# 108 extra TensorE products behind the last real one, with forward or backward moving operand and weights at step one or two

## The chip, the cores and the metric

The kernel runs on one core of one Trainium2 chip. That core has a TensorE for matrix products (PE in the profile, with its weight loads as PEld), VectorE (DVE), ScalarE (ACT), GpSimd (POOL) and SyncE (SP), which mostly issues transfers. Products read two operands from the on-chip memory SBUF, a weight block of up to 128 columns that is loaded into the array and a moving operand that streams past it, and write into PSUM, which has eight banks. The metric is the device time of one execution in microseconds (us); less is better.

## The reference

A decoder trunk of two layers on 256 tokens of width 1024, in float32. Layer 0 mixes tokens by forgetting attention, layer 1 by block-sparse attention with a shared position bias; each is followed by a SwiGLU network and a gated embedding. A final norm closes it.

```python
def reference(x, p, ...):
    h = x
    for i in range(DEPTH):
        u = _rmsnorm(h, attn_norm_g[i])
        ...
        h = h + _merge_heads(o) @ w_o[j]
        u = _rmsnorm(h, ffn_norm_g[i])
        gu = u @ ffn_w_in[i]
        h = h + (jax.nn.silu(gu[..., :D_FF]) * gu[..., D_FF:]) @ ffn_w_out[i]
        gate = jax.nn.sigmoid(_rmsnorm(h, ple_norm_g[i]) @ ple_w_gate[i])
        h = h + gate * (p[i] @ ple_w_up[i])
    return _rmsnorm(h, final_norm_g)
```

The change concerns the last two lines for layer 1, the gate and the final norm.

## The kernel before

For the large matrices, every float32 operand is split into two rounded parts, a high one and a rest (`hi` and `lo`), and every product of two such operands is made as three TensorE products into the same bank: high by high, high by low, low by high. That is `mm3` (lines 98 to 102); its three products appear in the profile as L100, L101 and L102. ScalarE makes the high part of a weight tile (`whi`, L188), VectorE the rest (`wlo`, L189), from a tile `raw` that SyncE fetches. The normed activations of a stage are the tile `g`: for each of 8 feature blocks 256 high values and behind them 256 low ones.

A weight tile is made by `half(at)` (line 144). It holds 1024 weights per partition in a tile that is 128 elements longer, and `at` says how many elements from the tile's start they begin. Where they begin differs by stage: `blocks` uses 16 (`APART`), the last stage 48.

The last stage is `ple` for layer 1 (from line 836 on). Its gate product is computed with tokens as rows: 128 tokens of `g` are the weights of the array, and the gate's matrix is the moving operand. First come the columns 0 to 511 for both token halves, in bank pairs `bks[0]`; then the columns 512 to 1023 for the first 128 tokens at 512 columns a product (`pair_unit` with `bks[1]`); then those for the second 128 tokens in two quarters of 256 columns (`tokens`, into `bks[1][1]` and into the bank `own`, named `pg_own` in the profile). Behind the last quarter stand six products into the bank `uown` (`pu_own`), the embedding's part of that quarter. The four weight tiles of this stage are the list `wts`; `nm.both` is `g`.

When a quarter is done, `part(t, i)` applies the gate (ScalarE's sigmoid, L844, VectorE's products and sums, L845 and L846), sums the squares for the final norm (L868 or L890) and multiplies by the last gain. `root` takes the root on GpSimd (L905), the rows are scaled (L912, L914, L928 to L932) and stored (`rows`, L902). All PSUM tiles come from one pool of eight banks in rotation (`bank`). Engines run in the order in which the program is written, apart from places where `tc.issue_after(x)` holds a piece back until `x` has been issued; the order of TensorE's last products is fixed in this way. At the end of the program (L1046) all engines meet in a barrier.

The extra products of the change read `wts[1]` as weights and `g` as moving operand.

Of the kernel before, what the change touches and what calls it, by code (L numbers as in the profile page):

```python
# [15 lines left out]
P = 128  # L16
S = 256
# [45 lines left out]
APART = 16  # L63
# [10 lines left out]
    ((2, 8), (0, 0), 0), ((0, 0), (2, 8), 64)  # L74
FORMS = {(_l, 0, _j): _HI2 for _l in range(2) for _j in (0, 4, 6)}
FORMS.update({(_l, "wo", _n): _HI2 for _l in range(2) for _n in (0, 2, 4)})
AGAIN = tuple((f, 0) for f in range(4, SEVEN + 4, 2))


# [2 lines left out]
def trunk(ctx: ExitStack, tc: tile.TileContext, pt, w, cst, gf, out):  # L82
# [7 lines left out]
    def bank(name):  # L90
        return ps.tile([P, 512], F32, tag="bank", name=name)
# [4 lines left out]
    mm = nc.tensor.matmul  # L96

    def mm3(o, a, b, start, stop):
        (ah, al), (bh, bl) = a, b
        mm(o, ah, bh, start=start, stop=False, skip_group_check=True)  # L100
        mm(o, ah, bl, start=False, stop=False, skip_group_check=True)  # L101
        return mm(o, al, bh, start=False, stop=stop, skip_group_check=True).ins  # L102
# [108 lines left out]
    def blocks(entry=False, form=None):  # L211

        if form:
            return half(APART, 0, form)
        hi, lo = half(APART, ENTRY * P if entry else 0)
        hi = [hi[:, k * P:(k + 1) * P] for k in range(KT)]
        return hi, lo if entry else [lo[:, k * P:(k + 1) * P] for k in range(KT)]
# [78 lines left out]
    nm = Norm(0)  # L296
# [9 lines left out]
    first = [half() for _ in range(EARLY)]  # L306
# [18 lines left out]
    def tokens(o, x, t, w, start, stop):  # L325

        at = slice(t * P, (t + 1) * P)
        return mm3(o, (x[0][:, at], x[1][:, at]), w, start, stop)

    def pair_unit(bks, c, wt, x, ts=(0, 1), mid=None):  # L330

        for kk in range(2):
            k = 2 * c + kk
            if kk and mid:
                mid()
            for t in ts:
                tokens(bks[t], x(k), t, [w[:, kk * HC:(kk + 1) * HC] for w in wt], k == 0, k == KT - 1)
# [252 lines left out]
    def ffn(layer, nm, filler, np_):  # L590
# [3 lines left out]
        def up(fs):  # L594
# [25 lines left out]
            for a in range(2):  # L620
                wt = blocks(form=_BOTH1 if (fs[0], a) in AGAIN else None)
                for k in range(KT):
# [152 lines left out]
    token = {}  # L775
# [60 lines left out]
    def ple(layer, nm, ut, nx):  # L836
# [4 lines left out]
        def gate(bk, t, c0, c1, u=None):  # L841
            at = slice(c0, c1)
            sg = work.tile([P, HC], F32, tag="t2k", bufs=3, name=f"pgt{layer}_{t}_{c0}")[:, 0:c1 - c0]
            nc.scalar.activation(sg, bk[:, c0 % HC:(c1 - 1) % HC + 1], AF.Sigmoid, scale=nm.col[:, t:t + 1])  # L844
            nc.vector.tensor_tensor(sg, sg, ut[:, t, at] if u is None else u, op=ALU.mult)  # L845
            nc.vector.tensor_tensor(h[:, t, at], h[:, t, at], sg, op=ALU.add)  # L846
# [17 lines left out]
        def square(t, i, c0, c1):  # L864

            sq = work.tile([P, S], F32, tag="sg", name=f"sqf{t}_{i}") if i else \
                work.tile([P, HC], F32, tag="t2k", bufs=3, name=f"sqf{t}_{i}")
            nc.scalar.activation(sq[:, 0:c1 - c0], h[:, t, c0:c1], AF.Square, scale=D ** -0.5,  # L868
                                 accum_out=ss[:, t, i:i + 1])

        for t in range(2):
# [3 lines left out]
        wts = [half(3 * APART) for _ in range(4)]  # L875
        uraw, uhi, ulo = [work.tile([P, 2, S], F32R if i else F32, tag="qkt", bufs=4, name=f"u{i}") for i in range(3)]
        nc.sync.dma_start(uraw, bass.AP(tensor=w.tensor, offset=w.offset + w_at(UP) + HC + S,
                                        ap=[[HW, P], [P * HW, 2], [1, S]]))
        with tc.issue_after(begun):
            split(uhi, ulo, uraw)  # L880
        uown = bank("pu1_own")
        own = bank(f"pg{layer}_own")

        def part(t, i):
            c0 = HC + i * S
            at = slice(c0, c0 + S)
            gate(own if t and i else bks[1][t], t, c0, c0 + S, uown[:, 0:S] if t and i else None)
            if t:
                sq = work.tile([P, S], F32, tag="sg", name=f"sqf1_{1 + i}")
                nc.vector.tensor_tensor_reduce(sq, h[:, t, at], h[:, t, at], 1.0 / D, ms[:, t, i:i + 1],  # L890
                                               ALU.mult, ALU.add, col[:, 1:2] if i else ms[:, t, 1:2])
            else:
                square(t, 1 + i, c0, c0 + S)
                if i:
                    nc.gpsimd.tensor_tensor(col[:, 0:1], ss[:, t, 2:3], ms[:, t, 1:2], op=ALU.add)
                else:
                    nc.vector.tensor_tensor(ms[:, t, 1:2], ms[:, t, 0:1], ss[:, t, 1:2], op=ALU.add)
            if not (t and i):
                nc.vector.tensor_tensor(ys[:, t, at], h[:, t, at], gb[:, at], op=ALU.mult)
# [4 lines left out]
        def root(t):  # L904
            nc.gpsimd.tensor_tensor(col[:, t:t + 1], col[:, t:t + 1], nhalf[:, 0:1], op=ALU.pow)  # L905

        for c in range(4):
            pair_unit(bks[1], c, wts[c], nm.k, (0,))
        part(0, 0)
# [6 lines left out]
        for i in range(2):  # L916
            for k in range(KT):
                c0 = (k % 2) * HC + i * S
                done = tokens((own if i else bks[1][1])[:, i * S:(i + 1) * S], nm.k(k), 1, [w[:, c0:c0 + S] for w in wts[k // 2]],
                       k == 0, k == KT - 1)  # L920
            if i:
                with tc.issue_after(done):
                    for k in range(2):
                        tokens(uown[:, 0:S], [p[:, k] for p in token["p"]], 1, (uhi[:, k], ulo[:, k]), k == 0, k == 1)
            part(1, i)
        root(1)
        r = col[:, 1:2]
        nc.scalar.activation(ys[:, 1, 0:HC], ys[:, 1, 0:HC], AF.Copy, scale=r)  # L928
# [6 lines left out]
    for layer in range(2):  # L935
        nf = Norm(3 * layer + 1)
        if layer == 0:
            attention(0, nm, fox_bias, first, nf)
        else:
            attention(1, nm, lambda _: (lambda: moba[2]), [], nf)  # L940
        got = []
        np_ = Norm(3 * layer + 2)
        ffn(layer, nf, lambda pp=None: ple_in(layer) if pp is None else got.append(ple_up(layer, pp)), np_)
        nm = Norm(3) if layer == 0 else None
        ple(layer, np_, got[0], nm)
# [104 lines left out]
```

## Time and profile before

| | us |
|---|---|
| median of 2 runs | 638.59 (638.58 to 638.59) |
| the profiled execution, its time | 638.56 |
| the profiled execution, its span from first to last instruction | 636.4 |

The profile is one execution. Its page gives the busy time of each engine, the chain of work that ended last, and groups of instructions. A group is named by line, engine, operation, what it writes and what it reads, and its shape. The timeline lists instructions with their start and duration in us, and in brackets how long the engine had idled and for whom. Products of TensorE overlap: a row's duration runs from its start to a modelled end, so the pace of a series is the distance between the starts. "SPq" rows are issues on SyncE's queue, and "DMA issues" give the time from an issue to its landing.

| engine | busy us | share of the span |
|---|---|---|
| TensorE, products | 629.4 | 99% |
| TensorE, weight loads (beside the products) | 608.4 | 96% |
| VectorE | 515.2 | 81% |
| ScalarE | 402.7 | 63% |
| GpSimd | 16.3 | 3% |

### The profile page before, as it was taken

The page shows a single profiled execution, that of the slowest core. Times are in us where ns is not written, and L with a number is a line of the kernel's source. Part 1 is how long each engine was busy: PE and PEld are TensorE (multiplying, and loading weights), DVE is VectorE, ACT ScalarE, POOL GpSimd, SP SyncE. Part 2 cuts the span into 40 slices and gives each one's busy share as a digit, 9 for nine tenths or more (in the row PEclk, how much of TensorE's full clock was granted, in tenths as well). Part 3 has the DMA queues.
Part 4 walks back from the last instruction along what each step waited for, and adds up shares of the span by engine and source line. Part 5 has one row for each costly group of instructions (what it writes and reads, how often), then busy time and mean ns, then how long its engine had stood idle before and what let it go on. Part 6 is the DMA issues. An engine that isn't in the chain of part 4 may idle for free.

```text
span 636.4 us, 13306 instructions
## 1 busy us (share of the span) xinstructions
PE 629.4 (99%) x5268; PEld 608.4 (96%) x5268; DVE 515.2 (81%) x968; ACT 402.7 (63%) x729; POOL 16.3 (3%) x33
## 2 busy tenths in 40 slices
PE   9999999999999999999999999999999999999996
PEld 7899999999999999999989999999999999999985
DVE  6987985899878788959996787678987888779765
ACT  8857675766555456558875486558655554465772
POOL 2500000000000000000000000000000000000002
PEclk9999999999999999999999999999999999999998
DMA  8889754267555568765687544426666664578601
GB/s 334 311 272 365 229 154 146 74 204 228 185 179 195 175 201 277 236 206 166 207 282 247 177 161 133 133 67 188 203 205 200 199 188 157 184 244 268 219 2 66
DMA packets 37214, 125.20 MB, mean 197 GB/s; under 512 B 3968, under 2 KB 7072, under 8 KB 37152
## 3 DMA queue, kind: packets, MB, share of 16 engines
q1 hardware_dynamic: 36832, 123.91, 59.3%
q8 instruction: 41, 0.67, 0.4%
q10 hardware_dynamic: 320, 0.44, 0.2%
q14 instruction: 21, 0.17, 0.1%
HBM read 123.25 MB, written 4.24 MB: 200 GB/s over the span
## 4 chain that ended last, share of the span: by engine, by line
PE 98%; POOL 0%; issue 0%; DVE 0%; ACT 0%; POOLq 0%; DVEq 0%
PE gu L102 13%; PE gu L101 13%; PE gu L100 13%; PE pq L100 5%; PE pq L101 5%; PE pq L102 5%; PE fo L102 4%; PE fo L101 4%; PE fo L100 4%; PE wo L100 2%; PE wo L102 2%; PE wo L101 2%; PE fs L102 2%; PE fs L101 2%; PE fs L100 2%; PE pg L101 2%
## 5 line engine op out<-in xcount | busy, mean ns | idle before, releaser
L189 DVE TENSOR_TENSOR wlo<-raw,whi 128x1024 fp32r<-128x1024 f32 (+1 forms) x170 | 202.2, 1195 | 35.3 <-ACT whi L188 35.0
L188 ACT ACTIVATE whi<-raw 128x1024 fp32r<-128x1024 f32 (+1 forms) x170 | 173.5, 1033 | 62.6 <-issue 20.8
L100 PE MATMUL gu<-g,whi 128*128 128x256 f32 x702 | 194.1, 277 | 0.0
L102 PE MATMUL gu<-g,wlo 128*128 128x256 f32 x702 | 194.0, 276 | 0.0
L101 PE MATMUL gu<-g,whi 128*128 128x256 f32 x702 | 193.9, 276 | 0.0
L102 PEld LDWEIGHTS gu<-g,wlo 128*128 128x128 f32 x702 | 131.9, 188 | 0.0
L100 PEld LDWEIGHTS gu<-g,whi 128*128 128x128 f32 x702 | 131.8, 188 | 0.0
L101 PEld LDWEIGHTS gu<-g,whi 128*128 128x128 f32 x702 | 131.8, 188 | 0.0
L100 PE MATMUL pq<-g,whi 128*128 128x256 f32 x256 | 71.1, 278 | 0.0
L102 PE MATMUL pq<-g,wlo 128*128 128x256 f32 x256 | 70.8, 276 | 0.0
L101 PE MATMUL pq<-g,whi 128*128 128x256 f32 x256 | 70.7, 276 | 0.0
L100 PE MATMUL fo<-fh,whi 128*128 128x256 f32 x224 | 61.9, 276 | 0.0
L102 PE MATMUL fo<-fh,wlo 128*128 128x256 f32 x224 | 61.9, 276 | 0.0
L101 PE MATMUL fo<-fl,whi 128*128 128x256 f32 x224 | 61.8, 276 | 0.0
L169 DVE TENSOR_TENSOR wlo<-raw,whi 128x128 fp32r<-128x128 f32 (+1 forms) x68 | 45.4, 686 | 12.1 <-ACT whi L164 12.1
L164 ACT ACTIVATE whi<-raw 128x128 fp32r<-128x128 f32 (+1 forms) x68 | 39.5, 622 | 23.9 <-PE pq L101 6.6
L100 PEld LDWEIGHTS pq<-g,whi 128*128 128x128 f32 x256 | 48.1, 188 | 1.1 <-issue 0.7
L101 PEld LDWEIGHTS pq<-g,whi 128*128 128x128 f32 x256 | 48.1, 188 | 0.1
L102 PEld LDWEIGHTS pq<-g,wlo 128*128 128x128 f32 x256 | 48.1, 188 | 0.0
L102 PEld LDWEIGHTS fo<-fh,wlo 128*128 128x128 f32 x224 | 42.1, 188 | 0.0
L100 PEld LDWEIGHTS fo<-fh,whi 128*128 128x128 f32 x224 | 42.1, 188 | 0.0
L101 PEld LDWEIGHTS fo<-fl,whi 128*128 128x128 f32 x224 | 42.1, 188 | 0.0
(216 smaller groups left out, 1271.2 us busy)
## 6 DMA issues: line engine op xcount, KB each, us to landing
raw<-w SPq DMA_DIRECT2D x212, 512.0 KB, 4.4
d<-d SPq DMA_DIRECT2D x4, 768.0 KB, 9.0
raw<-w SPq DMA_DIRECT2D x8, 256.0 KB, 4.5
bias<-d SPq DMA_DIRECT2D x4, 512.0 KB, 6.8
bias<-cd SPq DMA_DIRECT2D x2, 768.0 KB, 7.6
gx<-w SPq DMA_DIRECT2D x1, 512.0 KB, 5.4
bias<-cd SPq DMA_DIRECT2D x1, 512.0 KB, 7.4
p<-pt SPq DMA_DIRECT2D x2, 256.0 KB, 3.8
```

The source lines that it names most:

```text
L100: mm(o, ah, bh, start=start, stop=False, skip_group_check=True)
L101: mm(o, ah, bl, start=False, stop=False, skip_group_check=True)
L102: return mm(o, al, bh, start=False, stop=stop, skip_group_check=True).ins
L164: nc.scalar.activation(o, raw[:, c], AF.Copy)
L169: nc.vector.tensor_tensor(t[:, a + b0 * P:a + b1 * P], raw[:, b0 * P:b1 * P], f32(ht[:, a0:a0 + (b1 - b0) * P]), op=ALU.subtract)
L188: nc.scalar.activation(hi[:, c], raw[:, c], AF.Copy)
L189: nc.vector.tensor_tensor(lo[:, c], raw[:, c], f32(hi[:, c]), op=ALU.subtract)
```

## The change

Behind the last real product, 108 further products are issued. They write into a new bank `spare`, from column 0 to 255, each with `start=True`, so each overwrites the one before. Nothing reads that bank. There are 12 groups (`GROUPS`) of 9 products. A group says whether the moving operand is read backward (step minus one from its last element) or forward, with which step the 128 weights are read (one or two elements), and at which element of the weight tile they begin. The 9 products of a group follow the pattern of three `mm3`: for each of three feature blocks two products with the same weights, on the high and on the low half of `g`, and a third on the high half again, with weights one element further on where the step is two.

```diff
+GROUPS = ((0, 1, 80), (0, 2, 80), (0, 2, 48), (1, 1, 80)) + tuple((1, 2, i) for i in (64, 80, 96, 48, 72, 88, 104, 56))
...
+        spare = bank("spare")
+
+        def extra():
+
+            hi = wts[1][0]
+
+            def column(first, step):
+                return bass.AP(tensor=hi.tensor, offset=hi.offset - 3 * APART + first, ap=[list(hi.ap[0]), [step, P]])
+
+            x = nm.both.rearrange("p k i s -> p (k i s)")
+            for back, step, at in GROUPS:
+                for n in range(9):
+                    k, again, odd = n // 3, int(n % 3 == 1), int(n % 3 == 2)
+                    m0 = (2 * k + again) * S
+                    moving = bass.AP(tensor=x.tensor, offset=x.offset + m0 + (S - 1 if back else 0),
+                                     ap=[list(x.ap[0]), [-1 if back else 1, S]])
+                    mm(spare[:, 0:S], column(at + k * 256 + (step - 1) * odd, step), moving, start=True, stop=True,
+                       skip_group_check=True)
+
...
-                        tokens(uown[:, 0:S], [p[:, k] for p in token["p"]], 1, (uhi[:, k], ulo[:, k]), k == 0, k == 1)
+                        done = tokens(uown[:, 0:S], [p[:, k] for p in token["p"]], 1, (uhi[:, k], ulo[:, k]), k == 0, k == 1)
             part(1, i)
+        with tc.issue_after(done):
+            extra()
         root(1)
```

The groups in their order, as (direction, step, first element): forward 1 at 80; forward 2 at 80 and 48; backward 1 at 80; backward 2 at 64, 80, 96, 48, 72, 88, 104 and 56. So 27 products go forward and 81 backward, 18 have weights at step one and 90 at step two.

TensorE's order at the end of the program, before. Each row is line, operation, what it writes and reads, its columns, and what it waits for; `u` and `phi`, `plo` are the embedding's operands:

```order
L102 MATMUL pg_own<-whi_8224,g_5603 128x256
L100 MATMUL pu_own<-u_8230,phi_7445 128x256 [waits PE_49]
L101 MATMUL pu_own<-u_8231,phi_7445 128x256 [waits DVE_49]
L102 MATMUL pu_own<-u_8230,plo_7446 128x256
L100 MATMUL pu_own<-u_8230,phi_7445 128x256
L101 MATMUL pu_own<-u_8231,phi_7445 128x256
L102 MATMUL pu_own<-u_8230,plo_7446 128x256
L1046 UNCONDITIONAL_BRANCH
```

The same place in the changed kernel, whose lines are numbered one to 22 higher:

```order
L101 MATMUL pu_own<-u_8230,phi_7445 128x256
L102 MATMUL pu_own<-u_8231,phi_7445 128x256
L103 MATMUL pu_own<-u_8230,plo_7446 128x256
L924 MATMUL spare<-g_5603,whi_8212 128x256 [waits PE_49]
L924 MATMUL spare<-g_5603,whi_8212 128x256 x107
L1068 UNCONDITIONAL_BRANCH
```

The added rows stand between the last `pu_own` product and the end of the program. The first waits for an earlier product of TensorE; the 107 others wait for nothing. No instruction of VectorE, ScalarE, GpSimd or SyncE has moved.

## The prediction
> **What bounds the kernel now.** I read the page's busy table first, then the chain of work that ended last, then the end of the timeline, because the change adds its work there.
>
> ```profile
> span 636.4 us, 13306 instructions
> PE 629.4 (99%) x5268; PEld 608.4 (96%) x5268; DVE 515.2 (81%) x968; ACT 402.7 (63%) x729; POOL 16.3 (3%) x33
> ...
> PE 98%; POOL 0%; issue 0%; DVE 0%; ACT 0%; POOLq 0%; DVEq 0%
> ```
>
> TensorE is busy for 99% of the span and carries 98% of the chain, so work put between its products would lengthen the kernel one for one. This work stands behind the last product, though, and there TensorE is idle. The timeline's rows (start, duration, engine, line, operation) around the last real product, and behind them the rows of the closing instructions (line 1046) on SyncE's queue with the waits of that queue:
>
> ```profile
> 629.18 0.28 PE L102 MATMUL pg_own<-whi,g 128*128 128x256 f32 x1
> 629.29 0.28 PE L100 MATMUL pu_own<-u,phi 128*128 128x256 f32 x1
> ...
> 629.88 0.28 PE L102 MATMUL pu_own<-u,plo 128*128 128x256 f32 x1
> 630.27 0.42 DVE L845 TENSOR_TENSOR pgt<-pgt,pu_own 128x256 f32<-128x256 f32 x1 [0.29 <-PE pu_own L102]
> ...
> 632.74 0.81 SPq L902 DMA_DIRECT2D out<-end  x2
> ...
> out<-end SPq DMA_DIRECT2D x2, 128.0 KB, 2.1
> ...
> SPq L1046 <- DMA out<-end: 1.7, 2, 0.9
> ...
> L1046 SPq DRAIN  x3: 7/7/7, 635.7 to 636.0; - x3
> ```
>
> The last real product starts at 629.88 and ends at 630.16. Behind it come the gate, the square root, the scaling and the last store, whose two issues end at 632.74 + 0.81 = 633.55. The store lands about 2.1 us later, near 635.65; SyncE waits for it, and its first closing drain stands at 635.7. From that drain to the end of the span is 636.4 - 635.7 = 0.7 us of closing barrier, which every engine must reach. So TensorE has 635.7 - 630.16 = 5.5 us of room between its last product and the barrier. Work behind the last product is free up to that; beyond it, every microsecond counts in full.
>
> **The change part by part.** It adds a bank of PSUM (`spare`) and 108 products of 256 columns: 12 groups of 9. It removes nothing. 27 products read the moving operand forward and 81 backward; 18 read the weights with step one and 90 with step two. TensorE's order ends with them, behind the last pair for `pu_own`; on the other queues nothing is moved, and no DMA is added, so the last store issues and lands when it did.
>
> *The wait.* The first product waits for an earlier product of TensorE itself, because of the bank. That product is ahead of it in the same queue, so I cost the wait at nothing; the five `pu_own` rows below, whose first also waits for a product, show no gap. Behind the waiting product stand only the other 107 and the end of the program.
>
> *The rate of a product.* What counts is the distance from start to start, not the 0.28 us of a row, as products overlap. These timeline rows give it in the last stages:
>
> ```profile
> 612.12 0.39 PE L100 MATMUL pg<-whi,g 128*128 128x512 f32 x1
> ...
> 618.24 0.39 PE L100 MATMUL pg<-whi,g 128*128 128x512 f32 x1
> ...
> 623.84 0.28 PE L100 MATMUL pg<-whi,g 128*128 128x256 f32 x1
> ...
> 626.57 0.28 PE L100 MATMUL pg_own<-whi,g 128*128 128x256 f32 x1
> ```
>
> From 626.57 to 629.29 there are 24 products of 256 columns: 2.72 / 24 = 0.1133 us each. From 629.29 to 629.88 there are five steps between `pu_own` products: 0.59 / 5 = 0.118. The products of 512 columns take (618.24 - 612.12) / 27 = 0.2267 in the first half, exactly twice 0.1133, and (623.84 - 618.24) / 24 = 0.2333 in the second half, whose operands lie at other places. So the pace follows the columns that stream, and the place of the operands moves it by 3 to 4%. With step one and forward I take 0.1133; the first group, which is that, costs 9 x 0.1133 = 1.02 us.
>
> *Weights with step two (90 products).* No row shows a strided weight load. The nearest rows for a load as the limit are the transposes, which stream only 128 columns:
>
> ```profile
> 374.14 2.13 PE L533 MATMUL pp<-cs,e 128*128 128x128 f32 x18
> ...
> L533 PE MATMUL pp<-cs,e x18: 272/272/273, 374.1 to 376.0; 128*128 128x128 f32 x18
> ...
> L100 PEld LDWEIGHTS pg_own<-whi,g x8: 187/188/188, 626.5 to 628.8; 128*128 128x128 f32 x8
> ```
>
> Less the last one's duration, 17 steps take 2.13 - 0.27 = 1.86 us, 0.109 each, although 128 columns at the pace above would need 0.057. A load of 128 columns therefore seems to need up to 0.109, close under the 0.1133 of the stream. That leaves 4 ns of slack: if step two slows the load, it shows at once. The lower end is 0.109 per product. The upper end is a load at half rate, 2 x 0.109 = 0.218. A load's own record lasts 0.188, but loads start every 0.113, so that is no pace.
>
> *Moving operand backward (81 products).* No row shows that either. The only operands in the trace that are not read with step one are those of the nine warm-up products, which read one element again and again (step zero) on both sides:
>
> ```profile
> 0.76 3.91 PE L133 MATMUL cold<-const-float32-0.0 128*128 128x512 f32 x9 [0.76 <-PEq L1042]
> ...
> 4.28 0.38 PE L133 MATMUL cold<-const-float32-0.0 128*128 128x512 f32 x1
> 4.61 0.49 PE L452 MATMUL v<-whi,g 128*128 128x512 f32 x1
> ...
> L133 PEld LDWEIGHTS cold<-const-float32-0.0 x9: 286/336/336, 0.7 to 3.9; 128*128 128x128 f32 x9
> L133 PE MATMUL cold<-const-float32-0.0 x9: 382/634/764, 0.8 to 4.3; 128*128 128x512 f32 x9
> ```
>
> From the first (0.76) to the ninth (4.28) are eight steps of 3.52 / 8 = 0.44 us, against 0.2267 later: half the rate. Read as the price of a step other than one, that is 0.22 per 256 columns, the upper end for this edit (the lower end is 0.109 again). But the ninth product has the same operands as the others, and the next one starts only 4.61 - 4.28 = 0.33 later; its record is 0.38 like the unit-step rows at 612 us, where the median of the nine is 0.63. The slowness went away with time, not with the operands. So I take the low value, 0.1133, for both edits: the evidence of half rate is explained without the step.
>
> The Trainium skill (page "TensorE: Matmul & The Clock Gate", Part 1) says that the array's clock is halved until about 3.4 us of sustained activity, which would be this start; the profile's clock line does not show it there, but its durations agree. By the halving as a price of the step the sum would end near 655, by the clock's halving at 645.4. The Trainium skill (page "SBUF — State Buffer", "SBUF cachelines") also says that reads are at full bandwidth if a line of 16 bytes is hit at least twice in a row; by that four-byte elements at step two or backward would cost nothing, but two hits are just the limit, and no run here shows it.
>
> *The sum.* The first added product starts at 629.88 + 0.12 = 630.00, the last 107 x 0.1133 = 12.12 us later, at 642.12, and ends at 642.40. SyncE's drain follows within 0.1 us, the end of the span 0.7 later: 643.2, against 636.4. That is 6.8 us more, not 12.2, since 5.5 us are idle before the barrier today. The profiled execution took 638.56 with its span of 636.4, so 2.1 us lie around it; it stands 0.03 under the median of 638.59. The result is 638.6 + 6.8 = 645.4, that is 1.1% more. I count changes within 2% (625.8 to 651.4) as no change.
>
> **The rivals.**
>
> *A reading at half rate: slower.* If step two halves the weight load, 90 products cost 0.218 in place of 0.1133: 9.4 us more, 654.8. If going backward halves the stream, 81 products do (0.22 each): 8.6 more, 654.0; both together, 99 products, 656. For it: the warm-up's 0.44, and a load with 4 ns of slack. Against it: the ninth warm-up product. It decides (over 651.4) from 6.0 / 90, 0.067 us, more per product of step two, that is from 0.18 each.
>
> *A partial price.* The two readings of the weights and the moving operand get in each other's way more often, as the 0.2333 and 0.118 above show at some places. At 0.118 throughout, the sum is 0.5 more, 645.9; at a third more (0.15) for the 90, 3.3 more, 648.7.
>
> *A cheaper stream, or products that stay under the cover.* At the 0.109 of the load, the sum is 0.5 us less, 644.9. To vanish under the 5.5 us before the barrier, 108 products would have to run at 0.051 each, under half of any row of 256 columns; the time would then stay at 638.6. All 108 are in the order and none leaves out its weight load, so I give that next to nothing.
>
> **How the numbers follow.** The forecast, all products between 0.109 and 0.12 (644.9 to 646.2), has 0.70, and within it 0.1133 gives 645.4. The partial price (646.2 to 651.4) has 0.13, the half rate (over 651.4) 0.16, no effect 0.01. The range that leaves out no more than 2 in 10 is 644.6 to 650: the forecast with its lower bound and some rounding of the rows, and most of the partial price. Faster by over 2% has next to no way, as nothing is removed: 0.01. Slower by over 2% is the half rate: 0.16. The rest, 0.83, is within 2%.
>
> **What would show it.** Right: in the changed kernel's timeline 108 `spare` products follow from 630.0 on without a gap, about 0.113 apart in every group, the last starting at 642.1; the last store still issues near 632.7 to 633.2; SyncE's closing drain stands right behind TensorE's last product, at 642.5, and the span is 643.2. Wrong: groups whose distances differ, above all the first nine (forward, step one) against the next eighteen (step two) and the fourth group (backward, step one); a distance near 0.22 in either would be the half rate. A gap ahead of the first `spare` product would refute the free wait, and a drain that follows TensorE by more than 0.1 us the fixed close of 0.7.

## The result and the profile after

| | us | against the kernel before |
|---|---|---|
| before, median of 2 runs | 638.59 | |
| changed, median of 2 runs | 646.34 (646.23 to 646.45) | 1.0119 (95% interval 1.0103 to 1.0136) |
| the same kernel again, median of 4 | 646.18 (645.99 to 646.78) | 1.0119 (1.0105 to 1.0133), before: 638.77 (638.18 to 639.71, 15 runs) |

The kernel became 1.2% slower. On the page of the changed kernel, the added products take the whole end of the chain of work:

```profile
span 644.4 us, 13522 instructions
...
PE 642.8 (100%) x5376; PEld 621.5 (96%) x5376; DVE 515.6 (80%) x968; ACT 402.4 (62%) x729; POOL 17.3 (3%) x33
...
PE 100%; issue 0%
```

TensorE has 5376 products, 108 more than before, and 13.4 us more busy time, while the span has grown by 8.0. The timeline at the end of the changed kernel (start, duration, engine, line, operation, count), then the closing instructions on SyncE's queue and its waits (in total, times, longest):

```profile
630.50 0.28 PE L103 MATMUL pu_own<-u,plo 128*128 128x256 f32 x1
630.62 12.95 PE L924 MATMUL spare<-g,whi 128*128 128x256 f32 x108
...
633.36 0.81 SPq L903 DMA_DIRECT2D out<-end  x2
...
L1068 SPq DRAIN  x3: 7/7/7, 643.6 to 643.9; - x3
...
SPq L1068 <- PE spare L924: 5.4, 1, 5.4
```

The 108 products follow without a gap and end at 630.62 + 12.95 = 643.57. The last store's issues end at 634.17, as long behind the last real product as before. SyncE, which used to wait last for that store, now waits 5.4 us for the added products; its drain follows at 643.6, and the span ends 0.8 later.

Two things differ from the forecast. The mean distance of the 108 is (12.95 - 0.28) / 107 = 0.1184 us, not 0.1133; and the last real product starts at 630.50, not at 629.88. The distance differs by group. These rows keep to one way of reading each, in order: all of the first group (forward, step one), 17 of the 18 products of the second and third (forward, step two), eight of the fourth (backward, step one), and most of the eight groups with both, behind the fourth's last product:

```profile
630.62 1.20 PE L924 MATMUL spare<-g,whi 128*128 128x256 f32 x9
...
631.78 2.21 PE L924 MATMUL spare<-g,whi 128*128 128x256 f32 x17
...
633.83 1.10 PE L924 MATMUL spare<-g,whi 128*128 128x256 f32 x8
...
634.77 7.61 PE L924 MATMUL spare<-g,whi 128*128 128x256 f32 x63
```

Less the last product's 0.28 and divided by the steps: 0.115, 0.1206, 0.117 and 0.1182. No group is near the 0.22 of half rate; all but the first stand 3 to 6% above 0.1133.

The 0.62 by which the main part ends later arises in the first microseconds. There the first four real products took 1.19 us before and 1.61 in the changed kernel's profile, and they started later:

```profile
4.61 1.19 PE L452 MATMUL v<-whi,g 128*128 128x512 f32 x4
```

```profile
4.81 1.61 PE L453 MATMUL v<-whi,g 128*128 128x512 f32 x4
```

### The profile page after: what moved, and what is told of

It reads as the page before. It is cut to its first block, busy times and chain, and to the rows that moved or that the text cites. A ratio compares the mean times of both kernels' runs of the same rounds, so it can differ in the third digit from the quotient of the medians.

```text
span 644.4 us, 13522 instructions
## 1 busy us (share of the span) xinstructions
PE 642.8 (100%) x5376; PEld 621.5 (96%) x5376; DVE 515.6 (80%) x968; ACT 402.4 (62%) x729; POOL 17.3 (3%) x33
## 4 chain that ended last, share of the span: by engine, by line
PE 100%; issue 0%
PE gu L102 12%; PE gu L101 12%; PE gu L103 12%; PE pq L101 5%; PE pq L102 5%; PE pq L103 5%; PE fo L101 4%; PE fo L102 4%; PE fo L103 4%; PE wo L101 2%; PE wo L103 2%; PE wo L102 2%; PE pg L102 2%; PE pg L103 2%; PE pg L101 2%; PE fs L103 2%
```

## The experiments

In all but the first, `extra` goes through a list `PRODUCTS` of (first element, step and columns of the moving operand, first element and step of the weights). Where a diff shows `GROUPS`, the list is made from it; its entries are then (backward or not, step of the weights, their first element, columns, number of products). Operands, bank and place behind the last real product stay as in the change unless the diff says otherwise. Diffs are against the changed kernel and show only the lines that matter; `...` stands for what is left out. Only unused products differ; what the kernel computes is untouched.

**Is the late start part of the change?** The changed kernel without an edit.

> The changed kernel once more, as it is. Its profile of before this run had 108 products at a mean distance of 118.4 ns, and its main part ended 0.62 us later than in the profile of the kernel before. If that delay is chance of one start, the time here is 645.4 plus 0.5 for the pace, 645.9, or up to 646.4; if the change causes it, it is 646.3 again in every round, and the main part again ends near 630.5.

It took 646.18, 7.41 over the kernel before in the same rounds. Its last real product starts at 630.13, between the 629.88 and 630.50 of the earlier profiles:

```profile
630.13 0.28 PE L103 MATMUL pu_own<-u,plo 128*128 128x256 f32 x1
630.25 12.95 PE L924 MATMUL spare<-g,whi 128*128 128x256 f32 x108
```

The 15 runs of the kernel before also spread over 1.5 us, and its profiled execution, with 638.56, was quicker than their median of 638.77. In the profiles of the runs below that add products behind the last real one, that product starts anywhere from 629.97 to 630.93, and 45 products added there leave the median where it was (below). So the late start is chance of one execution, and the change itself costs 7.4: the 6.8 of the forecast and 0.55 for the pace, (0.1184 - 0.1133) x 107, together 7.35.

**Does the way of reading set the pace?**

```diff
-GROUPS = ((0, 1, 80), (0, 2, 80), (0, 2, 48), (1, 1, 80)) + ...
+GROUPS = ((0, 1, 80, 256, 108),)
```

> All 108 products forward, with weights at step one from element 80; nothing else differs from the changed kernel. If the way of reading sets the pace (my theory), they stand 0.1133 us apart and the time is 0.5 us under that of the changed kernel in the same rounds. If any product behind the end is slower (the one bank written again and again, the weights from one tile), the distance stays at 0.118 and the times are equal.

```profile
631.03 12.42 PE L931 MATMUL spare<-g,whi 128*128 128x256 f32 x108
```

(12.42 - 0.28) / 107 = 0.1135: the same bank, tile and place with plain operands run at the forecast's pace. The 0.53 us by which this series is shorter is what was expected; of the times it shows as 0.36 (645.82 against 646.18, ratio 1.0112, 1.0098 to 1.0126, against 1.0119), within their spread. So it is not standing behind the end that makes the products of the change slower; how they are read makes the difference between these two kernels, which start behind the same `pu_own` products.

**Is the room behind the last product free, and only there?** The same 45 plain products, once behind the last real product and once ahead of `pu_own`.

```diff
+GROUPS = ((0, 1, 80, 256, 45),)
```

```diff
                 with tc.issue_after(done):
+                    done = extra()
+                with tc.issue_after(done):
                     for k in range(2):
                         done = tokens(uown[:, 0:S], ...)
...
-        with tc.issue_after(done):
-            extra()
```

> Only 45 products, forward and step one, behind the last real one: 45 x 0.1133 = 5.1 us, which fits into the 5.5 us between the last product and the closing barrier. If the room behind the last product is free (my theory), the time is that of the kernel before, 638.6, within 0.3. If added work counts in full wherever it stands, it is 5.1 more, 643.7.

> The same 45 products, put between the last product for pg_own and the first for pu_own, so that the six pu_own products and all that follows them wait. My theory: they count in full there, 638.6 + 5.1 = 643.7. If the place does not matter, the time equals that of the run with the 45 behind the last real product.

Behind, they cost nothing: 638.71, ratio 1.0001 (0.9992 to 1.0010). Ahead, the same products cost 5.27: 644.04, ratio 1.0084 (1.0070 to 1.0098). The timeline and SyncE's last wait of the run with the 45 behind, and then the timeline of the run with them ahead:

```profile
630.38 5.28 PE L931 MATMUL spare<-g,whi 128*128 128x256 f32 x45
...
SPq L1075 <- DMA out<-end: 1.7, 2, 0.9
```

```profile
629.83 5.46 PE L931 MATMUL spare<-g,whi 128*128 128x256 f32 x45
635.12 0.28 PE L114 MATMUL pu_own<-u,phi 128*128 128x256 f32 x1
```

Behind, TensorE is done at 635.66, and SyncE still waits last for the store. Ahead, `pu_own` and all behind it starts 5.3 later. One thing was not expected: the same 45 products have a distance of (5.28 - 0.28) / 44 = 0.1136 behind and (5.46 - 0.28) / 44 = 0.1177 ahead, with the same operands.

**Place, size and step.** Three kernels with 216 products each, of which only the distances are read.

```diff
+GROUPS = ((0, 1, 48, 256, 18), (0, 1, 56, 256, 18), ..., (0, 1, 104, 256, 18), (1, 1, 48, 256, 18), (1, 1, 64, 256, 18), (1, 1, 80, 256, 18), (1, 1, 104, 256, 18))
```

> Twelve groups of 18 products of 256 columns with weights at step one: eight forward, whose weights begin at elements 48, 56, 64, 72, 80, 88, 96 and 104, then four backward at 48, 64, 80 and 104. If the direction sets the pace, all forward groups stand at 0.1133 us and all backward ones at 0.118. If the place of the weights does, the groups differ with the first element, up to 0.120, in both directions. What counts are the distances, not the time (216 products: about 638.6 + 24.7 - 5.5 = 658).

It took 658.48. Forward from 48, from 80 and from 88, and backward from 80:

```profile
630.20 2.16 PE L931 MATMUL spare<-g,whi 128*128 128x256 f32 x17
...
638.69 1.98 PE L931 MATMUL spare<-g,whi 128*128 128x256 f32 x16
640.74 2.08 PE L931 MATMUL spare<-g,whi 128*128 128x256 f32 x16
...
651.47 2.05 PE L931 MATMUL spare<-g,whi 128*128 128x256 f32 x16
```

Forward they stand at 0.1175, 0.1133 and 0.120, backward at 0.118. Plain forward products are as slow as backward ones from most places; of the eight, only the stretch from 80 ran at 0.1133. The expectation that direction alone sets the pace fell. That the place sets it is not shown either: each place stood behind one other group only, and the next runs show that this matters.

```diff
+GROUPS = ((0, 1, 80, 512, 18), (0, 2, 80, 512, 18), (1, 1, 80, 512, 18), (1, 2, 80, 512, 18), (0, 1, 80, 256, 18), ..., (1, 2, 80, 128, 18))
```

> Groups of 18 products of 512, 256 and 128 columns, each forward with weights at step one, forward at two, backward at one and backward at two, from element 80. If a load at step two is the limit (it takes 0.120 us by itself), 512 columns hide it (0.2267, as at step one) and 128 columns show it (0.120 against 0.109). If each load at step two holds up the stream beside it, it adds the same 7 ns at 512 and at 256 columns. If going backward costs per column, its 4.6 ns at 256 columns are 9 at 512 and 2 at 128; if per product, 4.6 at each.

It took 667.49. Rows at 512 columns (forward one, forward two, backward one), then the same three at 256 and at 128:

```profile
631.28 3.90 PE L931 MATMUL spare<-g,whi 128*128 128x512 f32 x16
635.71 3.84 PE L931 MATMUL spare<-g,whi 128*128 128x512 f32 x16
639.62 4.13 PE L931 MATMUL spare<-g,whi 128*128 128x512 f32 x17
...
648.03 1.87 PE L931 MATMUL spare<-g,whi 128*128 128x256 f32 x15
650.10 1.97 PE L931 MATMUL spare<-g,whi 128*128 128x256 f32 x15
652.25 1.93 PE L931 MATMUL spare<-g,whi 128*128 128x256 f32 x15
...
656.32 1.95 PE L931 MATMUL spare<-g,whi 128*128 128x128 f32 x16
658.34 2.05 PE L931 MATMUL spare<-g,whi 128*128 128x128 f32 x16
660.56 1.84 PE L931 MATMUL spare<-g,whi 128*128 128x128 f32 x15
```

At 512 columns (0.39 for the last one) the distances are 0.234, 0.230 and 0.234: neither step two nor backward costs anything, though the plain products did not reach the expected 0.2267 either. At 256 they are 0.1136, 0.121 and 0.118. At 128 (0.27 to 0.28 for the last one) they are 0.112, 0.118 and 0.112: step two costs 6 ns, backward nothing. The plain 0.112 is nearly that of 256 columns, so at 128 something other than the stream sets the distance; taken as the load, it is 6 ns slower at step two, and 0.118 is more than the 0.1133 that 256 columns stream. That is argued, and explains more than half of the excess at 256 columns (0.121), not all of it. Going backward has no price per column and none per product, as it shows at 256 columns alone.

```diff
+STEPS = ((1, 1), (2, 1), (4, 1), (8, 1), (-1, 1), (-2, 1), (-4, 1), (1, 2), (1, 4), (1, 8), (2, 2), (4, 4))
+PRODUCTS = [(n // 3 % 3 * 512 + (-255 * ms if ms < 0 else 0), ms, S, 48 + (ws > 1 and n % 3 == 2), ws)
+            for ms, ws in STEPS for n in range(18)]
```

> Groups of 18 products of 256 columns: moving operand at step 1, 2, 4, 8, -1, -2 and -4 with weights at step one; weights at step 2, 4 and 8 with the moving operand at step one; both at 2; both at 4. By the rule of 16-byte lines (Trainium skill, page SBUF - State Buffer, cachelines) steps of one and two elements run at full rate and steps of four and eight are slowed. If the price follows the number of 64-byte pieces that are touched, it grows in proportion: each doubling of the step doubles the excess over 0.107 us. If only the columns count, all stand at 0.113.

`STEPS` holds the step of the moving operand and that of the weights. It took 677.41. The timeline's rows for both at step one, the moving operand at step 2, 4, 8, -1 and -2, then the weights at 2, 4 and 8, and the durations in ns of all its products (least, median, most):

```profile
630.37 1.93 PE L920 MATMUL spare<-g,whi 128*128 128x256 f32 x15
632.46 4.09 PE L920 MATMUL spare<-g,whi 128*128 128x256 f32 x17
636.60 4.14 PE L920 MATMUL spare<-g,whi 128*128 128x256 f32 x17
641.00 3.66 PE L920 MATMUL spare<-g,whi 128*128 128x256 f32 x16
644.74 1.96 PE L920 MATMUL spare<-g,whi 128*128 128x256 f32 x15
646.88 3.92 PE L920 MATMUL spare<-g,whi 128*128 128x256 f32 x16
...
655.39 1.96 PE L920 MATMUL spare<-g,whi 128*128 128x256 f32 x15
657.55 4.13 PE L920 MATMUL spare<-g,whi 128*128 128x256 f32 x17
661.76 4.04 PE L920 MATMUL spare<-g,whi 128*128 128x256 f32 x16
...
L920 PE MATMUL spare<-g,whi x216: 276/409/441, 630.1 to 674.1; 128*128 128x256 f32 x108
```

With about 0.4 taken off for the last product of a slow row and 0.28 for that of a fast one, both at step one stand at 0.118, the moving operand at 0.230, 0.233, 0.218, 0.120 and 0.233, the weights at 0.120, 0.233 and 0.242. So half rate exists: about twice the 0.1133 of the fastest plain products. The moving operand falls to it at once with any step of two or more, in either direction, and then stays there. The weights fall to it from step four. By the rule of 16-byte lines (the Trainium skill, "SBUF — State Buffer", "SBUF cachelines") four-byte elements at step two run at full rate. For weights these rows nearly agree (0.120, the same as other plain rows); for the moving operand they contradict it, 0.230 against 0.118 at step one from the same place, and the measurement decides. Proportion to the pieces touched fell as well: 4 and 8 are no slower than 2.

**What decides between 0.1133 and 0.118?** Two kernels: eight stretches of 27 equal products, each behind one that differs; and the 45 plain products in the middle of `pu_own`, in the path as in the run ahead, but with a `pu_own` product in front as in the run behind.

```diff
+LEADS = ((0, 1, 48), (0, 1, 56), (0, 1, 64), (0, 1, 88), (0, 1, 96), (0, 1, 104), (1, 1, 80), (0, 2, 80))
+PRODUCTS = []
+for back, step, at in LEADS:
+    PRODUCTS.append((S - 1 if back else 0, -1 if back else 1, S, at, step))
+    PRODUCTS += [(..., 1, S, 80 + n % 9 // 3 * 256, 1) for n in range(27)]
```

```diff
-                with tc.issue_after(done):
-                    for k in range(2):
-                        done = tokens(uown[:, 0:S], ...)
+                for k in range(2):
+                    with tc.issue_after(done):
+                        done = tokens(uown[:, 0:S], ...)
+                    if k == 0:
+                        with tc.issue_after(done):
+                            done = extra()
...
-        with tc.issue_after(done):
-            extra()
```

> Eight stretches of 27 products that are all alike (256 columns, forward, weights at step one from element 80), each behind one product that is different: weights from 48, 56, 64, 88, 96 or 104, or backward, or step two. If only the way and place of reading set the distance, all eight stretches settle at 0.1133 within a few products. If what runs ahead decides which of several steady distances a stretch falls into (my theory, since the same 45 products stood at 0.1134 behind pu_own and at 0.1179 ahead of it), some stretches stay at 0.1175 to 0.118 to their end.

> The 45 products between the third and the fourth pu_own product. They have a pu_own product ahead of them, as in the run with the 45 behind, but stand in the path, as in the run with the 45 ahead. If what runs ahead decides the distance, it is 0.1134 here, and the time is 5.1 us over the kernel before. If the place in the program does (the other engines' work beside it, or what follows), it is 0.118 and 5.3 us.

They took 659.57 and 644.44. The stretches behind the leads 104 and backward, then the 45 in the middle:

```profile
647.24 3.00 PE L922 MATMUL spare<-g,whi 128*128 128x256 f32 x25
650.54 3.11 PE L922 MATMUL spare<-g,whi 128*128 128x256 f32 x25
```

```profile
630.46 5.26 PE L931 MATMUL spare<-g,whi 128*128 128x256 f32 x45
```

The same 27 products stand at (3.00 - 0.28) / 24 = 0.1133 behind one lead and at 0.1179 behind the other, to their end. Behind 56, 96 and 104 they settle at 0.1133, behind the other five at 0.1175 to 0.118. In the middle of `pu_own` the 45 have 0.1132. So these products have two steady distances, and what runs ahead chooses between them, not the place in the program. The time of the run in the middle is 5.98 over the kernel before in its round, not the expected 5.1; its first `pu_own` product started at 630.11, 0.82 later than in the profile of the kernel before, which is about the difference.

**Has the way of reading a price of its own?**

```diff
+LEADS = (56, 96, 104, 48)
+WAYS = ((0, 1), (1, 1), (0, 2), (1, 2))
+PRODUCTS = []
+for back, step in WAYS:
+    for at in LEADS:
+        PRODUCTS += [(512 * n, 1, S, at + n * 256, 1) for n in range(3)]
+        PRODUCTS += [(..., -1 if back else 1, S, 80 + ..., step) for n in range(15)]
```

> Sixteen stretches of 15 products from element 80 (forward step one, backward step one, forward step two, backward step two; four stretches of each), each behind three forward products with weights at step one from 56, 96, 104 or 48. If going backward or step two has a price of its own, no lead-in brings those stretches to 0.1133, and they stand at 0.1175 or more behind all four. If it is only that their lead-in put them into the slower of two steady distances, some of them stand at 0.1133, as forward step one does behind 56, 96 and 104.

`WAYS` holds (backward, step of the weights). It took 667.41. One stretch of each way, in that order:

```profile
637.20 1.87 PE L925 MATMUL spare<-g,whi 128*128 128x256 f32 x15
641.73 1.57 PE L925 MATMUL spare<-g,whi 128*128 128x256 f32 x12
650.13 1.73 PE L925 MATMUL spare<-g,whi 128*128 128x256 f32 x13
660.87 1.58 PE L925 MATMUL spare<-g,whi 128*128 128x256 f32 x12
```

They give 0.1136, 0.1173, 0.121 and 0.118. Forward at step one settled at 0.1133 behind three of its four leads, 56, 104 and 48, and at 0.118 behind 96. In the run before it was 48 that gave the slower distance and 96 the faster one, behind a single lead product instead of three; so the first element of the lead does not decide by itself. Backward at step one stayed between 0.117 and 0.118 behind all four, forward at step two at 0.120 to 0.121, and both together near 0.118. So within these leads, no backward or step-two stretch reached the faster distance.

## Why the prediction was right

The forecast was 645.4, the range 644.6 to 650, "within 2%" at 0.83; 646.3 came. By its steps:

- **The room behind the last product.** Right, and shown from both sides: 45 products cost nothing behind (1.0001) and 5.27 us ahead. This term kept the cost at 7.4 us, where the products take 12.7.
- **The free wait, the unmoved store, the closing barrier.** Right for the wait, the issue and the close: there is no gap ahead of the first `spare` product, the store's issues keep their distance to the last real product, and the close takes 0.8 where 0.7 was assumed. That the store also "lands when it did" was wrong: it took 4.2 us in place of 2.1 (below). This cost nothing, as the products ran on until 643.57.
- **The pace of 0.1133.** Right for plain products (0.1135), too low for these by 0.005, or 0.55 us in all. The step of the forecast that was mis-sized is the one that gave both edits "the low value, 0.1133": 90 products at step two and the 9 others that go backward measured 0.117 to 0.121. So the sign of being wrong that it named, groups whose distances differ, did come, at 3 to 6%, and the smallest form of its rival "A partial price" (0.118 throughout, 645.9) describes the pace better than its forecast. The forecast had the rows (0.118 for `pu_own`, 3 to 4% by place) and set them aside for its single number. Its reading that the place of the operands makes these 3 to 4% is not borne out: the same 45 products, from the same places, had 0.1136 and 0.1177. Nor does any run show that the two readings get in each other's way, as that rival has it.
- **Step two.** "If step two slows the load, it shows at once" fits what came: 0.118 against 0.112 at 128 columns, 6 ns and not half rate.
- **Half rate as the rival.** It did not come, but the reason given against it was too weak. The ninth warm-up product only showed that step zero is not slow; the run over steps shows that a moving operand at step two runs at 0.230. By that distance, an estimate: had the change put its step two on the moving operand in 90 products, they alone would have cost 90 x 0.1167 = 10.5 us more, over the 2%. That step two stood on the weights, which bear it, was luck as far as the forecast's reasons go.
- **The start.** The main part of the changed kernel's profile was 0.62 late by chance, which no term could hold; it accounts for that execution's 646.45, where the forecast's sum with the measured pace gives 645.9. By it the median also lies just above the 646.2 up to which the forecast's main case reached, while the mean distance of 0.1184 lies within that case's 0.109 to 0.12.

What stays open is why there are two steady distances, what in the products ahead chooses between them, and whether some lead would put backward products into the faster one; only four were tried for it.

## What to carry to other kernels

Work behind the last product of the bounding engine is free until that engine meets the closing barrier, and costs in full beyond it: read that room off the timeline (last product, last store, first drain) before costing anything there. Test an unusual access pattern on the operand that it is for: weights and moving operand take a step quite differently. Compare series of products by the distance of their starts, and do so with the same products in front.

## What the runs showed of the hardware that was not expected

- A series of products of 256 columns (forward, step one, weights from 80) has two steady distances, 0.1133 and 0.1177, and keeps the one into which the products ahead of it put it, the slower one for 45 products on end in one run. Other ways and places also stood at 0.117 to 0.121.
- A moving operand at any step of two or more in size runs at half rate (0.218 to 0.238 for 256 columns); at step minus one it runs at the slower of the usual distances (0.117 to 0.120).
- The last stores landed later in some runs: in the profiled changed kernel the 128 KB stores took 4.2 us where they took 2.1 before. TensorE running on behind them is not enough for it: with products of 512 columns behind (the run over sizes) they took 2.1. What goes with it in the traces is a transfer of 16 KB that the profile calls an instruction transfer (queue `q8` of the DMA view). In the six profiles with 3.0 to 4.2 it ran among the stores, in the changed kernel from 634.5 to 636.1; in the run over sizes it came at 637.6, behind them; in the run over steps it began as they ended, at 635.7, and they took 2.4; in the kernel before and the three runs with 45 products none ran there, and they took 2.1. No run was made to show that it is the cause, and the delay was hidden behind the products.

The changed kernel, and then the run over sizes:

```profile
q8 instruction: 1, 0.02, 0.6%
...
out<-end SPq DMA_DIRECT2D x2, 128.0 KB, 4.2
```

```profile
q8 instruction: 1, 0.02, 0.3%
...
out<-end SPq DMA_DIRECT2D x2, 128.0 KB, 2.1
```
